# A hybrid stream step on one core: five kept weight units, a fixed order on three engines and grouped transpositions between output and up projection, and another bank for a pool tile

## The chip, the core and the metric

The kernel runs on one core of a Trainium2 chip. Its engines are called as in the profile: PE is TensorE (matrix products; PEld is its weight load), DVE is VectorE, ACT is ScalarE, POOL is GpSimd, SP is SyncE, which here only issues transfers. The metric is the device time of one execution in microseconds (us). Time before is the median of three executions.

## The reference, cut to what matters

One layer is computed for 384 tokens (256 of a prompt and 128 of eight running streams), with a model width of 2048 and a hidden width of 8192:

```python
u = rmsnorm(x, g_mix_pre);  proj = u @ w_in        # pool | z | xBC | dt | gates
a_pool = pool_mixer(...)                           # windows 2, 4, 8, 16
a_ssd  = gated_rmsnorm(ssd_scan(...), z)
m = sigmoid(gA) * (a_pool @ w_pool_proj) + sigmoid(gB) * (a_ssd @ w_ssd_proj)
x = x + rmsnorm(m @ w_out, g_mix_post)             # output projection
x = x + rmsnorm(square(relu(rmsnorm(x, g_mlp_pre) @ w_up)) @ w_down, g_mlp_post)
```

The change lies almost wholly in the last two lines, between `m @ w_out` and the first products with `w_up`. No result of `w_up` can be had before the norm over a token's whole row of `m @ w_out` is known.

## The kernel before, in words

**Products.** Every 32-bit operand is split in a high and a low part, `h` and `l`. A weight unit is 128 x 1024 numbers (512 KB): SP loads it (`wfetch`, L62 to L65), ACT rounds it to `wh` (L72), DVE subtracts to get `wl` (L74). There are three buffers each for the raw unit, `wh` and `wl`. One product is three PE instructions (`mm3`, L80 to L83): `wh` with the high part, `wh` with the low part, `wl` with the high part. `half` (L89) does eight such products with one unit, `proj` (L98) two or more units into one result tile.

**Result tiles.** There are eight banks: two are called `mm` (pool `psm`), six `ss` (pool `pss`). A tile waits until its bank has been read empty.

**Who orders the instructions.** The program is written in order, but a planner places the instructions on each engine by its own costs and due times; it may move one past another on the same engine where the data allow. Each engine then runs its list strictly in that order. `behind(ins)` pins the instructions in it after `ins` on the same engine; with `chain[0]` set, `half` pins each set of products after `last[0]`. Weight splits are not pinned, save the two that `hold` governs: the splits for the second half of up tile 0 and for up tile 1, which `gate` keeps behind the last square root on ACT and a residual on DVE.

**Pool tiles near the start.** Pool tiles 0, 1 and 2 are accumulated in `ss` banks, tile 3 (`ps3`, L246) and tile 4 in the two `mm` banks. The next product is `gate_a(0)` (`pj_ga`), then `pool_map(0)` (`pw`), which needs the four differences `dh`/`dl` of pool tiles 0 to 3 from ACT and DVE (L325, L326).

**End of the scan.** After the last group the program runs `dside`, `gate_b`, `state`, `gate_b`, and then the last transpositions and products of the scan. `state` (`su`, L668) multiplies `xst`, which makes a way through DRAM.

**Output projection.** `moving` (L845) keeps the activations in PE and streams 512 columns of weights. `w_out` is done in four column blocks `nb` of eight units; each gives three result tiles `o[b]`, one for each block `b` of 128 tokens. For `nb = 3` the last three units are kept (`tail = 3`) and used block after block, so that block 0 is done 36 instructions before block 2. `done(b)` squares and sums `o[b]` on ACT (L910), multiplies it with the norm's weights into `hm` on DVE (L913) and, for `nb = 3`, runs `postnorm` (L879 to L892): a root on ACT and eight small instructions on DVE. Ten residuals `x1 += hm * y` follow on DVE (L925), 512 columns each, and two on ACT and POOL (L922, L923).

**To the up projection.** For each of 16 slices `k` of 128 columns, PE transposes the three token blocks of `x1` into one `ss` bank (`trm`, L935), ACT scales and rounds to `x1h` (L939), DVE gets `x1l` (L940). These feed the 64 up tiles `pj_up`, each 48 PE instructions of 384 columns. The norm before the up projection is applied to its results: twelve squares (L951), three `postnorm`, a diagonal `dg` (L955), a product with ones (`bc`, L957, two instructions) and a copy to `r2` (L958). The first reader of an up tile (`ht`, L979) needs `r2`. `bc` lies ahead of up tile 2 in PE's order.

Of the kernel before, what the change touches and what calls it, by code (L numbers as in the profile page):

```python
# [34 lines left out]
def build(ctx, tc, io):  # L35
# [31 lines left out]
    def wsplit(f):  # L67
        w, name = f
        h = wpool.tile([P, 1024], F32R, tag="wh", name=f"wh_{name}")
        l = wpool.tile([P, 1024], F32R, tag="wl", name=f"wl_{name}")  # L70
        with behind(hold[0]):
            s.activation(h, w, AF.Copy)  # L72
        with behind(hold[1]):
            v.tensor_tensor(l, w, h.bitcast(F32), ALU.subtract)  # L74
        return h, l

    def wload(src, name):
# [160 lines left out]
    for k in range(2, KD, 2):  # L238
# [205 lines left out]
    with tc.tile_pool(name="phd", bufs=2, reuse_waits="tile") as pd, tc.tile_pool(  # L444
# [278 lines left out]
        for g in range(G + 1):  # L723
            if g == G:
                dside(prev.p[1])
                gate_b()
                state(prev.p[1])
                gate_b()
                py = sstile("pp_last")
                lump(lambda: t_yT(prev.p[1]))  # L730
                lump(lambda: t_Y(prev.p[1]))
                lump(lambda: t_pp(prev.p[1], py))
                final(prev.p[1])
                gate_b()
# [107 lines left out]
    x1 = res.tile([P, 3, DM], F32, name="x1")  # L842
    r2 = res.tile([P, T], F32, name="r2")

    def moving(o, units, lhs, tail, done, pool=None):  # L845
        nk = len(lhs)

        def mm(b, wh, wl, k, k2):
# [5 lines left out]
            te.matmul(o[b], ml, wh[:, c], start=False, stop=k == nk - 1)  # L854
# [7 lines left out]
        w = [wload(*units[kp]) for kp in range(n - tail, n - max(0, tail - 3))]  # L862
        for kp in range(n - max(0, tail - 3), n):
# [33 lines left out]
    with tc.tile_pool(name="phf", bufs=1, side="right", reuse_waits="tile") as pf, tc.tile_pool(  # L897
# [1 line left out]
    ) as pf2:  # L899
        hm = pf.tile([P, 3, DM], F32, name="hm")  # L900
        st = pf.tile([P, 3, 4], F32, name="st1")
        ys = []
        for nb in range(4):
            gpo = pf2.tile([P, 512], F32, tag="gpo", name=f"gpo{nb}")
            sy.dma_start(gpo, io["g_mix_post"][blk(nb)].partition_broadcast(P))
            o = [sstile(f"wo{nb}_{b}") for b in range(3)]

            def done(b):
                q = pf2.tile([P, 512], F32, tag="q", name=f"q1_{nb}_{b}")
                s.activation(q, o[b], AF.Square, accum_out=st[:, b, nb : nb + 1])  # L910
                if nb == 3:
                    ys.append(postnorm(pf2, st, b, "n1"))
                v.tensor_tensor(hm[:, b, blk(nb)], o[b], gpo, ALU.mult)  # L913

            moving(o, [(io["w_out"][nb, kp], f"wo{nb}_{kp}") for kp in range(8)], ms_, 3 if nb == 3 else 0, done)
        gate = [root[0], None]
        for i in range(4):
            for b in range(3):
                xb = x1[:, b, blk(i)]
                if b == 1 and i >= 2:  # L920
                    hb = hm[:, b, blk(i)]
                    s.activation(hb, hb, AF.Copy, scale=ys[b])  # L922
                    gp.tensor_tensor(xb, xb, hb, ALU.add)  # L923
                    continue
                ins = v.scalar_tensor_tensor(  # L925
                    out=xb, in0=hm[:, b, blk(i)], scalar=ys[b], in1=xb, op0=ALU.mult, op1=ALU.add
                )
            if i == 0:
                gate[1] = ins
    pga = ctx.enter_context(tc.tile_pool(name="pga", bufs=1, reuse_waits="tile"))  # L930
    xs2 = []
    for k in range(KD):
        tr = sstile(f"trm{k}")
        for b in range(3):
            te.transpose(tr[:, b * P : b * P + P], x1[:, b, k * P : k * P + P], ident)  # L935
        h = pga.tile([P, T], F32R, name=f"x1h{k}")
        l = pga.tile([P, T], F32R, name=f"x1l{k}")
        g1 = vec[:, V_GMLP + k : V_GMLP + k + 1]
        s.activation(h, tr[:, :T], AF.Copy, scale=g1)  # L939
        v.scalar_tensor_tensor(out=l, in0=tr[:, :T], scalar=g1, in1=h.bitcast(F32), op0=ALU.mult, op1=ALU.subtract)  # L940
        xs2.append((h, l))
    mpool.close()

    with tc.tile_pool(name="phg", bufs=1, reuse_waits="tile") as pg, tc.tile_pool(
        name="phg2", bufs=2, reuse_waits="tile"
    ) as pg2:
        st = pg.tile([P, 3, 4], F32, name="st2")
        for b in range(3):
            for i in range(4):
                q = pg2.tile([P, 512], F32, tag="q3", name=f"q2_{b}_{i}")  # L950
                s.activation(q, x1[:, b, blk(i)], AF.Square, accum_out=st[:, b, i : i + 1])  # L951
        dg = pg.tile([P, 3, P], F32, name="dg2")
        for b in range(3):
            y = postnorm(pg2, st, b, "n2")
            v.tensor_scalar(dg[:, b, :], ident, y, None, ALU.mult)  # L955
        bc = sstile("bc2")
        te.matmul(bc[:, :T], ones, dg.rearrange("p b t -> p (b t)"), start=True, stop=True)  # L957
        s.copy(r2, bc[:, :T])  # L958
# [5 lines left out]
        pg.tile([P, 96], F32, name="pad_e")  # L964
        NC = 8
        for c8 in range(NC):
            hh = []
            for f8 in range(8):
                f = c8 * 8 + f8
                if f == 0:  # L970
                    ps = mmtile("pj_up0")[:, :T]
                    half(ps, 0, wload(io["w_up"][0, 0], "up0_0"), xs2)
                    hold[:] = gate
                    half(ps, 1, wload(io["w_up"][0, 1], "up0_1"), xs2)
                else:
                    ps = proj([io["w_up"][f, 0], io["w_up"][f, 1]], xs2, f"up{f}")
                    hold[:] = [None, None]
                t = pg2.tile([P, T], F32, tag="t", name=f"ht{f}")
                v.scalar_tensor_tensor(out=t, in0=ps, scalar=0.0, in1=r2, op0=ALU.max, op1=ALU.mult)  # L979
                s.activation(t, t, AF.Square)  # L980
# [5 lines left out]
            for nb in range(4):  # L986
                o = [sstile(f"wd{c8}_{nb}_{b}") for b in range(3)]

                def done(b):
# [10 lines left out]
                        v.tensor_tensor(dst, dst, gpo[:, blk(nb)], ALU.mult)  # L1000
                        return
                    if b == 0:
                        pg.tile([P, 32], F32, name="pad_z")
# [14 lines left out]
                    4 if c8 == NC - 1 and nb == 3 else 0,  # L1018
                    done,
                    pg,  # L1020
                )


# [117 lines left out]
```

## Time and profile before

| what | us |
|---|---|
| median of three executions (2834.87 to 2838.39) | 2836.21 |
| profiled execution, its own time | 2834.49 |
| its span, from the first to the last instruction | 2832.7 |
| PE busy in the span | 2812.7 (99%) |
| DVE, ACT, POOL busy | 1562.9, 1092.0, 96.6 |
| granted PE clock, mean of the span | 0.998 |

Times in a timeline are counted from the start of the span. Matmuls overlap: a matmul of 384 columns is shown with 0.33 us but the next begins 0.173 us later, one of 512 columns is shown with 0.39 us and the next begins 0.227 us later, so work on PE is counted by starts. An "idle" in brackets stands ahead of the instruction that ended it, with what released it.

### The profile page before, as it was taken

The page shows a single profiled execution, that of the slowest core. Times are in us where ns is not written, and L with a number is a line of the kernel's source. Part 1 is how long each engine was busy: PE and PEld are TensorE (multiplying, and loading weights), DVE is VectorE, ACT ScalarE, POOL GpSimd, SP SyncE. Part 2 cuts the span into 40 slices and gives each one's busy share as a digit, 9 for nine tenths or more (in the row PEclk, how much of TensorE's full clock was granted, in tenths as well). Part 3 has the DMA queues.
Part 4 walks back from the last instruction along what each step waited for, and adds up shares of the span by engine and source line. Part 5 has one row for each costly group of instructions (what it writes and reads, how often), then busy time and mean ns, then how long its engine had stood idle before and what let it go on. Part 6 is the DMA issues. An engine that isn't in the chain of part 4 may idle for free.

```text
span 2832.7 us, 39399 instructions
## 1 busy us (share of the span) xinstructions
PE 2812.7 (99%) x15807; PEld 2673.1 (94%) x15807; DVE 1562.9 (55%) x2245; ACT 1092.0 (39%) x1582; POOL 96.6 (3%) x155
## 2 busy tenths in 40 slices
PE   9999999999999999999999999999999999999998
PEld 8999999999999999999999987989899998989897
DVE  6673335687887877886433335434444444444445
ACT  6342224445445445454422234433232333323233
POOL 0000000000000000011000000000000000000000
PEclk9999999999999999999999999999999999999999
DMA  7444445556655665656644543434333343433333
GB/s 263 134 129 141 141 139 193 184 182 203 205 190 193 200 200 190 226 179 229 194 149 149 167 162 111 134 127 127 131 128 127 127 127 129 131 127 127 127 128 125
DMA packets 143494, 451.40 MB, mean 159 GB/s; under 512 B 17296, under 2 KB 43216, under 8 KB 138320
## 3 DMA queue, kind: packets, MB, share of 16 engines
q1 hardware_dynamic: 135056, 412.96, 44.7%
q0 software_dynamic: 8256, 35.93, 3.5%
q8 instruction: 124, 2.03, 0.3%
q14 instruction: 58, 0.48, 0.1%
HBM read 407.11 MB, written 41.72 MB: 158 GB/s over the span
## 4 chain that ended last, share of the span: by engine, by line
PE 98%; DVE 1%; ACT 0%; DMA 0%; issue 0%; SPq 0%; DVEq 0%; ACTq 0%
PE pj_up L83 6%; PE pj_up L81 6%; PE pj_up L82 6%; PE wd L853 6%; PE wd L854 6%; PE wd L852 6%; PE pj_x L81 5%; PE pj_x L83 5%; PE pj_x L82 5%; PE pj_sp L82 3%; PE pj_z L81 3%; PE pj_z L82 3%; PE pj_sp L83 3%; PE pj_z L83 3%; PE pj_sp L81 3%; PE pj_ga L81 2%
## 5 line engine op out<-in xcount | busy, mean ns | idle before, releaser
L83 PE MATMUL pj_up<-x1h,wl_up 128*128 128x384 f32 x1024 | 342.8, 335 | 0.6 <-DVE wl_up L74 0.6
L81 PE MATMUL pj_up<-x1h,wh_up 128*128 128x384 f32 x1024 | 343.0, 335 | 0.0
L82 PE MATMUL pj_up<-x1l,wh_up 128*128 128x384 f32 x1024 | 342.8, 335 | 0.0
L74 DVE TENSOR_TENSOR wl_wd<-w_wd,wh_wd 128x1024 fp32r<-128x1024 f32 x127 | 155.7, 1226 | 261.9 <-ACT wh_wd L72 261.9
L853 PE MATMUL wd<-wl_wd,hh 128*128 128x512 f32 x762 | 296.6, 389 | 0.0
L854 PE MATMUL wd<-wh_wd,hl 128*128 128x512 f32 x762 | 296.6, 389 | 0.0
L852 PE MATMUL wd<-wh_wd,hh 128*128 128x512 f32 x762 | 296.2, 389 | 0.0
L72 ACT ACTIVATE wh_wd<-w_wd 128x1024 fp32r<-128x1024 f32 x127 | 134.8, 1061 | 350.7 <-PE wd L854 284.1
L74 DVE TENSOR_TENSOR wl_up<-w_up,wh_up 128x1024 fp32r<-128x1024 f32 x128 | 156.8, 1225 | 199.6 <-ACT wh_up L72 199.6
L72 ACT ACTIVATE wh_up<-w_up 128x1024 fp32r<-128x1024 f32 x128 | 135.8, 1062 | 326.4 <-PE pj_up L82 265.7
L81 PE MATMUL pj_x<-xgh,wh_x 128*128 128x384 f32 x768 | 257.4, 335 | 0.0
L82 PE MATMUL pj_x<-xgl,wh_x 128*128 128x384 f32 x768 | 256.6, 334 | 0.0
L83 PE MATMUL pj_x<-xgh,wl_x 128*128 128x384 f32 x768 | 256.6, 334 | 0.0
L83 PEld LDWEIGHTS pj_up<-x1h,wl_up 128*128 128x128 f32 x1024 | 192.3, 188 | 1.0 <-DVE wl_up L74 0.9
L81 PEld LDWEIGHTS pj_up<-x1h,wh_up 128*128 128x128 f32 x1024 | 192.5, 188 | 0.4
L82 PEld LDWEIGHTS pj_up<-x1l,wh_up 128*128 128x128 f32 x1024 | 192.5, 188 | 0.3
L81 PE MATMUL pj_z<-xgh,wh_z 128*128 128x384 f32 x512 | 171.1, 334 | 0.0
L83 PE MATMUL pj_z<-xgh,wl_z 128*128 128x384 f32 x512 | 171.1, 334 | 0.0
L853 PEld LDWEIGHTS wd<-wl_wd,hh 128*128 128x128 f32 x762 | 143.0, 188 | 29.7 <-DVE wl_wd L74 0.2
L854 PEld LDWEIGHTS wd<-wh_wd,hl 128*128 128x128 f32 x762 | 143.0, 188 | 29.7
L82 PE MATMUL pj_z<-xgl,wh_z 128*128 128x384 f32 x512 | 171.0, 334 | 0.0
L81 PE MATMUL pj_sp<-abh,wh_sp 128*128 128x384 f32 x512 | 171.0, 334 | 0.0
(305 smaller groups left out, 6088.0 us busy)
## 6 DMA issues: line engine op xcount, KB each, us to landing
w_up<-w_up SPq DMA_DIRECT2D x128, 512.0 KB, 3.4
w_wd<-w_down SPq DMA_DIRECT2D x128, 512.0 KB, 3.4
w_x<-w_in SPq DMA_DIRECT2D x96, 512.0 KB, 4.3
w_z<-w_in SPq DMA_DIRECT2D x64, 512.0 KB, 3.5
w_sp<-w_ssd SPq DMA_DIRECT2D x64, 512.0 KB, 3.5
w_ga<-w_in SPq DMA_DIRECT2D x32, 512.0 KB, 3.5
w_pp<-w_pp SPq DMA_DIRECT2D x32, 512.0 KB, 3.4
hs<-ssm SPq DMA_DIRECT2D x16, 1024.0 KB, 6.2
```

Of the source, the lines that this page charges most:

```text
L72: s.activation(h, w, AF.Copy)
L74: v.tensor_tensor(l, w, h.bitcast(F32), ALU.subtract)
L81: te.matmul(out, wh, xh, start=first, stop=False)
L82: te.matmul(out, wh, xl, start=False, stop=False)
L83: return te.matmul(out, wl, xh, start=False, stop=last)
L852: te.matmul(o[b], mh, wh[:, c], start=k == 0, stop=False)
L853: te.matmul(o[b], mh, wl[:, c], start=False, stop=False)
L854: te.matmul(o[b], ml, wh[:, c], start=False, stop=k == nk - 1)
```

## The change

Six things are edited.

1. Pool tile 3 is accumulated in an `ss` bank.
2. At the end of the scan both `gate_b` run before `state`.
3. In the last block of `w_out` five units are kept instead of three, all five with split tiles of their own (`own = 5`, pool `phk`), so that the three `wh`/`wl` buffers are free for three `w_up` units. The norm's weights are scaled by -0.5 on ACT, which makes `postnorm` one instruction shorter on DVE. Blocks 0 and 1 get their residuals, and block 0 its squares, as soon as they are done; all residuals are on DVE.
4. Transpositions are split into early ones (blocks 0 and 1, two slices to a bank, eight groups) and late ones (block 2, four slices to a bank, four groups), and so are the scalings that read them.
5. Up tiles 0 and 1 are computed together, slice by slice, with `hold` and `gate` gone; PE's order is pinned by `chain`, ACT's by `act`, DVE's by `dve`. Up tile 2 goes to an `ss` bank.
6. `bc` goes between the halves of up tile 2 and uses a high and a low part with rounded ones. The `pad` tiles change size so that later tiles keep their places.

```diff
-    hold = [None, None]
+    tail_pe = [None]
...
-        with behind(hold[0]):
-            s.activation(h, w, AF.Copy)
-        with behind(hold[1]):
-            v.tensor_tensor(l, w, h.bitcast(F32), ALU.subtract)
+        s.activation(h, w, AF.Copy)
+        v.tensor_tensor(l, w, h.bitcast(F32), ALU.subtract)
...
-    ps3 = mmtile("pj_p3")[:, :T]
+    ps3 = sstile("pj_p3")[:, :T]
...
                 dside(prev.p[1])
                 gate_b()
+                gate_b()
                 state(prev.p[1])
-                gate_b()
                 py = sstile("pp_last")
...
+            s.activation(gpo, gpo, AF.Copy, scale=-0.5)
             o = [sstile(f"wo{nb}_{b}") for b in range(3)]
             def done(b):
...
                 v.tensor_tensor(hm[:, b, blk(nb)], o[b], gpo, ALU.mult)
+                if nb < 3:
+                    return
+                ys[b] = postnorm(pf2, st, b, "n1", doubled=True)
+                if b == 2:
+                    return
+                for i in range(4):
+                    residual(b, i)
+                if b == 1:
+                    with behind(root[0]):
+                        for i in range(4):
+                            square(0, i)
+            moving(o, ..., 5 if nb == 3 else 0, done, pk, 5 if nb == 3 else 0)
...
+        ups = [mmtile(f"pj_up{n}")[:, :T] for n in range(2)]
+        uw = {n: wload(io["w_up"][n, q], f"up{n}_{q}") for n, q in ((0, 0), (1, 0))}
+        uw[2] = wload(io["w_up"][0, 1], "up0_1")
+        chain[0] = True
+        last[0] = lastwo
...
+        A, L = [early_turn(j) for j in range(5)], []
+        dve(lambda: residual(2, 0))
+        L.append(late_turn(0))
+        for g in range(4):
+            ks = range(4 * g, 4 * g + 4)
+            for k in ks:
+                hi(k, False)
+            if g:
+                act(lambda: square(1, g - 1))
+            for pair in ((ks[:2], ks[2:]) if g == 0 else (ks,)):
+                for k in pair:
+                    lo(k, False)
+                for k in pair:
+                    hi(k, True)
+                for k in pair:
+                    lo(k, True)
+            if g < 3:
+                dve(lambda: residual(2, g + 1))
+            def more():
+                A.append(early_turn(5 + g))
+                L.append(late_turn(g + 1))
+            if g == 0:
+                for k in ks:
+                    for n in range(2):
+                        prod(n, (k,), uw[n])
+                    if k == 2:
+                        more()
+            elif g == 1:
+                for k in (4, 5):
+                    for n in range(2):
+                        prod(n, (k,), uw[n])
+                more()
+                prod(0, (6, 7), uw[0])
+                prod(1, (6, 7), uw[1])
+                uw[3] = wload(io["w_up"][1, 1], "up1_1")
+            else:
+                for k in ks:
+                    prod(0, (k,), uw[2])
+                    if k == 10:
+                        more()
+        prod(1, range(8, KD), uw[3])
+        chain[0] = False
+        for b, i in ((1, 3), (2, 0), (2, 1), (2, 2), (2, 3)):
+            act(lambda: square(b, i))
...
+        ups.append(sstile("pj_up2")[:, :T])
+        half(ups[2], 0, wload(io["w_up"][2, 0], "up2_0"), xs2)
+        bc = sstile("bc2")[:, :T]
+        with behind(last[0]):
+            te.matmul(bc, onesr, dgh.rearrange("p b t -> p (b t)"), start=True, stop=False)
+            last[0] = te.matmul(bc, onesr, dgl.rearrange("p b t -> p (b t)"), start=False, stop=True)
+        with behind(last[0]):
+            half(ups[2], 1, wload(io["w_up"][2, 1], "up2_1"), xs2)
+        s.copy(r2, bc)
...
-                if f == 0:
-                    ps = mmtile("pj_up0")[:, :T]
-                    half(ps, 0, wload(io["w_up"][0, 0], "up0_0"), xs2)
-                    hold[:] = gate
-                    half(ps, 1, wload(io["w_up"][0, 1], "up0_1"), xs2)
-                else:
-                    ps = proj([io["w_up"][f, 0], io["w_up"][f, 1]], xs2, f"up{f}")
+                ps = ups[f] if f < 3 else proj([io["w_up"][f, 0], io["w_up"][f, 1]], xs2, f"up{f}")
```

`turn` (called by `early_turn` and `late_turn`) transposes the given token blocks of the given slices into one bank, pinned after `last[0]`. `hi(k, late)` is ACT's scaling of the two early blocks (256 columns) or of the late one (128 columns) of slice `k`, `lo(k, late)` DVE's difference for the same columns; `prod(n, ks, w)` is `mm3` for up tile `n` and the slices `ks`. Each is pinned after the one before it on its engine. The removed code is that of L918 to L941 and L948 to L958, told above.

More of the change, by code (lines that the diff above doesn't have):

```diff
@@ L843, in build, with moving @@
     r2 = res.tile([P, T], F32, name="r2")
-    def moving(o, units, lhs, tail, done, pool=None):
+    def moving(o, units, lhs, tail, done, pool=None, own=0):
         nk = len(lhs)
@@ L853, in mm @@
             te.matmul(o[b], mh, wl[:, c], start=False, stop=False)
-            te.matmul(o[b], ml, wh[:, c], start=False, stop=k == nk - 1)
+            tail_pe[0] = te.matmul(o[b], ml, wh[:, c], start=False, stop=k == nk - 1)
         n = len(units)
@@ L861, in moving @@
                     mm(b, wh, wl, kp * 2 + k2, k2)
-        w = [wload(*units[kp]) for kp in range(n - tail, n - max(0, tail - 3))]
-        for kp in range(n - max(0, tail - 3), n):
+        w = [wload(*units[kp]) for kp in range(n - tail, n - own)]
+        for kp in range(n - own, n):
             f, name = wfetch(*units[kp])
@@ L901, in build, with residual, square @@
         st = pf.tile([P, 3, 4], F32, name="st1")
-        ys = []
+        st2 = pf.tile([P, 3, 4], F32, name="st2")
+        phk = ExitStack()
+        pk = phk.enter_context(tc.tile_pool(name="phk", bufs=1, reuse_waits="tile"))
+        ys = [None] * 3
+        def residual(b, i):
+            xb = x1[:, b, blk(i)]
+            return v.scalar_tensor_tensor(
+                out=xb, in0=hm[:, b, blk(i)], scalar=ys[b], in1=xb, op0=ALU.mult, op1=ALU.add
+            )
+        def square(b, i):
+            q = pf2.tile([P, 512], F32, tag="q", name=f"q2_{b}_{i}", bufs=1)
+            return s.activation(q, x1[:, b, blk(i)], AF.Square, accum_out=st2[:, b, i : i + 1])
         for nb in range(4):
@@ L930, in build @@
[L930 to L941, printed above, removed]
+                if nb < 3:
+                    return
@@ new lines, in done @@
+                ys[b] = postnorm(pf2, st, b, "n1", doubled=True)
[7 more added lines that the diff above has]
+                            square(0, i)
+            moving(
+                o,
+                [(io["w_out"][nb, kp], f"wo{nb}_{kp}") for kp in range(8)],
+                ms_,
+                5 if nb == 3 else 0,
+                done,
+                pk,
+                5 if nb == 3 else 0,
+            )
@@ new lines, in build @@
+            lastwo = tail_pe[0]
+        phk.close()
+        pga = ctx.enter_context(tc.tile_pool(name="pga", bufs=1, reuse_waits="tile"))
+        xs2 = [
+            (pga.tile([P, T], F32R, name=f"x1h{k}"), pga.tile([P, T], F32R, name=f"x1l{k}")) for k in range(KD)
+        ]
+        ups = [mmtile(f"pj_up{n}")[:, :T] for n in range(2)]
+        uw = {n: wload(io["w_up"][n, q], f"up{n}_{q}") for n, q in ((0, 0), (1, 0))}
+        uw[2] = wload(io["w_up"][0, 1], "up0_1")
+        chain[0] = True
@@ new lines, in build, with turn, go, act @@
+        last[0] = lastwo
+        rt2 = root[0]
+        def turn(o, blocks, ks):
+            def go():
+                j = 0
+                for k in ks:
+                    for b in blocks:
+                        i = te.transpose(o[:, j * P : j * P + P], x1[:, b, k * P : k * P + P], ident)
+                        j += 1
+                return i
+            with behind(last[0]):
+                last[0] = go()
+        ca, cd = [rt2], [None]
+        def act(fn):
+            with behind(ca[0]):
+                ca[0] = fn()
@@ new lines, in dve, with part, hi @@
+        def dve(fn):
+            with behind(cd[0]):
+                cd[0] = fn()
+        def part(k, late):
+            i = k % 4 if late else k % 2
+            o = L[k // 4] if late else A[k // 2]
+            t = slice(TP, T) if late else slice(0, TP)
+            n = P if late else TP
+            g1 = vec[:, V_GMLP + k : V_GMLP + k + 1]
+            return o[:, i * n : i * n + n], xs2[k][0][:, t], xs2[k][1][:, t], g1
+        def hi(k, late):
+            src, h, l, g1 = part(k, late)
+            act(lambda: s.activation(h, src, AF.Copy, scale=g1))
@@ new lines, in lo, with early_turn, late_turn @@
+        def lo(k, late):
+            src, h, l, g1 = part(k, late)
+            dve(
+                lambda: v.scalar_tensor_tensor(
+                    out=l, in0=src, scalar=g1, in1=h.bitcast(F32), op0=ALU.mult, op1=ALU.subtract
+                )
+            )
+        def early_turn(j):
+            o = sstile(f"trm{j}")
+            turn(o, (0, 1), (2 * j, 2 * j + 1))
+            return o
+        def late_turn(i):
+            o = sstile(f"trl{i}")
+            turn(o, (2,), range(4 * i, 4 * i + 4))
+            return o
@@ new lines, in build @@
+        prod(1, range(8, KD), uw[3])
+        chain[0] = False
+        for b, i in ((1, 3), (2, 0), (2, 1), (2, 2), (2, 3)):
+            act(lambda: square(b, i))
+        dgh = pf.tile([P, 3, P], F32R, name="dgh2")
+        dgl = pf.tile([P, 3, P], F32R, name="dgl2")
+        with behind(cd[0]):
+            for b in range(3):
+                y = postnorm(pf2, st2, b, "n2")
+                v.tensor_scalar(dgh[:, b, :], ident, y, None, ALU.mult)
+                v.scalar_tensor_tensor(
+                    out=dgl[:, b, :], in0=ident, scalar=y, in1=dgh[:, b, :].bitcast(F32), op0=ALU.mult, op1=ALU.subtract
+                )
@@ L946, in build @@
     ) as pg2:
[L947 to L958, printed above, removed]
         hacc = pg.tile([P, 3, DM], F32, name="hacc")
@@ L1020, in build @@
                     pg,
+                    1 if c8 == NC - 1 and nb == 3 else 0,
                 )
```

30 lines of the change are left out of this document (11 added, 19 removed).

## The prediction

> **What bounds the kernel now.** I read the page's first part and its chain, then PE's waits, then the timelines of PE, DVE and ACT around each wait, and the clock there by stretch. PE works or is fed all the time:
>
> ```profile
> PE 2812.7 (99%) x15807; PEld 2673.1 (94%) x15807; DVE 1562.9 (55%) x2245; ACT 1092.0 (39%) x1582; POOL 96.6 (3%) x155
> ...
> PE 98%; DVE 1%; ACT 0%; DMA 0%; issue 0%; SPq 0%; DVEq 0%; ACTq 0%
> ```
>
> The change takes away no product, so it can only win where PE waits or runs slowly. PE's whole list of waits in the middle of the span is short:
>
> ```profile
> PE pj_ga L81 <- DVE pbuf L291: 3.5, 1, 3.5
> PE trm L935 <- DVE x L925: 2.4, 2, 2.0
> ...
> PE bc L957 <- DVE dg L955: 1.3, 1, 1.3
> PE su L668 <- DMA xst<-x_scr: 1.0, 1, 1.0
> PE pj_up L83 <- DVE wl_up L74: 0.6, 1, 0.6
> PE trm L935 <- DVE hm L913: 0.4, 1, 0.4
> ...
> PE trm L935 <- DVE x1l L940: 0.3, 1, 0.3
> ```
>
> Five of these seven are at the boundary from output to up projection and make 5.0 us; the pool tile has 3.5, the scan's end 1.0. The clock by stretch (columns: busy times, then the granted clock, DMA share, GB/s) shows one more loss:
>
> ```profile
> 1756.00:1758.00 2.00, 0.07 (x1) 0.00 (x0) 1.93 (x4) 1.37 (x2) 1.26 (x2) 0.81 0.08 33
> 1758.00:1760.00 2.00, 1.89 (x8) 1.67 (x8) 2.00 (x5) 1.37 (x3) 0.00 (x0) 0.50 0.00 0
> ...
> 1762.00:1764.00 2.00, 2.00 (x10) 1.85 (x9) 2.00 (x5) 1.53 (x5) 0.00 (x0) 0.50 0.98 406
> 1764.00:1766.00 2.00, 2.00 (x18) 1.93 (x16) 1.68 (x4) 1.78 (x4) 0.00 (x0) 0.99 0.20 82
> ```
>
> After the gap the granted clock is 0.50 for about 6.4 us. So I measure the boundary as a whole. ACT starts to read the last `w_out` tile at 1753.38; DVE reads up tile 2 at 1793.46:
>
> ```profile
> 1785.14 0.56 DVE L979 SCALAR_TENSOR_TENSOR ht<-pj_up,r 128x384 f32<-128x384 f32 x1 [1.55 <-PE pj_up L83]
> 1793.46 0.56 DVE L979 SCALAR_TENSOR_TENSOR ht<-pj_up,r 128x384 f32<-128x384 f32 x1 [2.02 <-PE pj_up L83]
> ```
>
> Both reads come 0.2 behind PE's last start, so the stretch is **40.1 us**, from 1753.18 (called T) on. Needed in it: three up tiles at 8.32 (the distance of these two rows), 24.96; 48 transpositions at 0.113 (three of them and a matmul take 0.51 in the timeline, less 0.173), 5.4; `bc` 0.4. That is 30.8, so 9.3 us are waits, slow clock and filling: the most that the boundary can give.
>
> **The change part by part, boundary.** *Ahead of T.* With five kept units block 1 ends 30 matmuls, 6.8 us, before T instead of 4.1. Its square, root, norm and four residuals of 0.67 take about 4.7 (block 0 now: 1745.2 to 1750.5 with three residuals and the table load of 1.3), so blocks 0 and 1 are ready before T. The five splits (1.06 on ACT, 1.23 on DVE each) need no PE release any more; by the issue times now (one unit each 4.08, landing in 3.4) the last is split some 20 us before T, and its first use is 15 before T. Hidden: ACT waits 3.0 of each 4.08 there. Four scalings of the norm's weights cost ACT 0.6 each in the same waits; the table load before the first root (1.28) stays ahead of T.
>
> *Block 2.* DVE's part after the root is what kept PE waiting:
>
> ```profile
> 1756.18 1.10 DVE L891 TENSOR_TENSOR n_n<-n_n,n_n 128x1 f32<-128x1 f32 x1
> 1757.31 1.41 DVE L925 SCALAR_TENSOR_TENSOR x<-hm,n_n,x 128x512 f32<-128x512 f32 x2
> ```
>
> L891 takes 0.15 elsewhere; here 1.10, while POOL's residual (1754.77 to 1757.26) runs, which the change drops, as it drops ACT's two scalings (0.71 each) ahead of the root. With the spacings of block 1 (square 0.7, root 0.3, DVE steps 0.2, 0.3, 0.2) the first residual starts at T+2.0 and ends at T+2.7, not T+4.9. PE fills this with 20 early transpositions: 0.138 each when alone (five in 0.69), 2.76; then four late ones, 0.55.
>
> *First product.* ACT's late scaling of slice 0 (128 columns; an estimate of 0.40 from 0.58 for 384 and 0.60 for 512) ends at T+3.9, DVE's difference at T+4.3. PE has done the transpositions at T+3.3, so 0.8 is idle. Now the first product starts at T+6.1 and then drips.
>
> *Pace after that.* A slice gives PE 1.04 (two tiles, six matmuls of 0.173). ACT needs 0.40 and 0.31 per slice, DVE 0.40 and 0.27, so both keep up, with three squares, four residuals and two or three splits in between. Where a late group is transposed, ACT and DVE need 0.3 to 0.7 until the next product. I follow the order group by group: groups 1 and 2 meet PE at about the time at which it is ready; in group 4 the early scalings of slices 14 and 15 wait for a transposition that PE does only after slice 10, a square stands behind them, and slice 12 comes 1.0 late. With a split of 1.06 on ACT in a bad place, 1.5.
>
> *Sum.* 3.3 + 0.8 + 24.96 + 24 transpositions at 0.13 (3.1) + `bc` 2 x 0.17 (0.35) + 1.5 = **34.0**. `bc` no longer waits: squares and norm end near T+25, PE asks for it at T+29. Gain **6.0**; bounds 3.5 (each of four groups 0.6 worse) and 7.5 (no group late).
>
> **Pool tile.** `pj_ga` could not start at 48.6 since both `mm` banks were held and DVE read tile 3 only at 51.7. With tile 3 elsewhere `pj_ga` runs at once. What is late next is `pool_map`, behind the same DVE:
>
> ```profile
> 56.80 0.55 DVE L326 TENSOR_TENSOR dl<-d,dh 128x384 fp32r<-128x384 f32 x1
> 57.27 0.69 DVE L306 TENSOR_TENSOR win<-win 128x516 f32<-128x516 f32 x1
> 57.88 1.22 DVE L74 TENSOR_TENSOR wl_pw<-w_pw,wh_pw 128x1024 fp32r<-128x1024 f32 x1
> ```
>
> `pj_ga` ends at 56.9; the fourth slice is wanted nine matmuls later, at 58.5; DVE has it at 57.3. The second `wl_pw` is wanted at 61.1 and there at 59.1. So the wait goes: gain **3.2** (lower bound 1.5, if the planner puts a window sum of 0.69 and a split of 1.22 ahead; upper 3.5). Six `ss` banks hold three pool tiles, tile 3 and `bc_x`; none is waited for.
>
> **Scan's end.** With 8.3 us more, `xst` is there: 1.0 goes. The second gate's units are split in time (1264.9 and 1278.7 for uses at 1275.9 and 1280.1). But the last transposition needs a seventh bank right behind `su`, so it waits for DVE's first state addition, perhaps behind a gate's product (0.55): 0.3. Gain **0.7**, bounds -0.3 and 1.0.
>
> **Sum.** 6.0 + 3.2 + 0.7 = 9.9. The profiled execution would go from 2834.5 to 2824.6; it lies 1.7 below the median of the runs, so the median would go from 2836.2 to **2826.3**.
>
> [...] The row is the 0.50 clock above, after 4.9 us with twelve transpositions and waits. A gap of 3.5 without any PE work (48.6 to 52.1) left the clock at 1.00, so the row alone doesn't say whether transpositions count. [...] No run here shows 24 transpositions in a row.
>
> **Rivals.**
> 1. *The clock halves after the 24 transpositions*, for 3.4 to 6.4 us (the row). Half of it is lost: 1.7 to 3.2, so 2828.0 to 2829.5. For: the row. Against: no gap over 0.7 is left, and the clock came back at 1764 after four products of 0.32 in 3.2 us. [...] 14%.
> 2. *The pool wait comes back as `pool_map` on DVE*, which is 9.9 of 10 us busy from 50 to 60: 1.7 lost, 2828.0. 8%.
> 3. *The order isn't what it says*: weight splits, `bc`'s copies and the scaling of `g_mlp_post` (1.92 on ACT) are not pinned; where the planner sets them between pinned ones, ACT blocks until PE frees a buffer. About 1.2 to 1.9 in each of three groups and half of the pool's gain gone: 2830.5 to 2835. 13%.
> 4. *Slower*: the clock stays at 0.50 through all four groups, since the products now come in lumps between transpositions. About 20 us of PE work (16.6 of products, 3.1 of transpositions) take twice as long: +18, less 9.9, so 2844. It decides from ten such microseconds on. Against: at 1760.8 to 1764 the products were sparser, and the clock rose. 5%.
>
> **How the numbers follow.** The forecast has 60%, at 2826.3. The low end takes all upper bounds (7.5 + 3.5 + 1.0 = 12.0) and 0.7 for the spread of the runs: 2823.5. The high end takes in rivals 1 and 2 and the edge of 3: 2831. About 2 in 10 are left out. 0.2% is 5.7 us, about what a measurement here can tell: faster by that is the forecast with rivals 1 and 2, 82%; within it rival 3, 13%; slower 5%.
>
> **What would show it.** Right: no wait of `pj_ga` on L291, none of `su` on `xst`; first residual of block 2 near T+2.0; first up product near T+4; `ht` of up tile 2 near T+34; clock 1.00 throughout. Wrong: a clock of 0.50 behind T, ACT waiting on PE ahead of a weight split within T to T+20, or a new wait of `pw` on `dl`.

## The result, and the profile after

The changed kernel takes **2826.31 us** (median of six executions, 2825.35 to 2827.09) against 2836.38 for the kernel before (six, 2834.87 to 2838.39): ratio 0.9964, 95% interval 0.9951 to 0.9977. The profiled execution took 2827.09, with a span of 2825.2, so it is one of the longer ones. The forecast was 2826.3. The number came out, but not all of its terms: the boundary gave less than forecast, the scan's end more, and in the medians the pool tile more too.

The page shows the same PE work in a shorter span:

```profile
PE 2811.2 (100%) x15807; PEld 2673.2 (95%) x15807; DVE 1565.7 (55%) x2263; ACT 1096.2 (39%) x1600; POOL 94.3 (3%) x153
...
PE 98%; DMA 1%; DVE 0%; ACT 0%; SPq 0%; issue 0%; DVEq 0%; ACTq 0%
```

The waits of PE after the change (total, times, longest). `pj_ga`, `su` and `bc` have left the list; apart from the first weights (`wh_e`, below), what stands in their place is all at the boundary and makes 2.9:

```profile
PE trl L963 <- DVE x L907: 1.1, 2, 0.9
...
PE pj_up L81 <- DVE wl_up L72: 0.7, 1, 0.7
PE pj_up L80 <- DVE x1l L995: 0.6, 2, 0.4
PE pj_up L79 <- ACT x1h L990: 0.5, 1, 0.5
```

The timeline of PE from T on (T is 1749.02 here, 0.2 before ACT's read of the last `w_out` tile at 1749.22) shows one block of 20 transpositions, a wait, four late ones, a wait, and the first product at T+4.3:

```profile
1748.96 2.34 PE L963 MATMUL trm<-cst,x 128*128 128x128 f32 x20
1752.17 0.66 PE L963 MATMUL trl<-cst,x 128*128 128x128 f32 x4 [0.86 <-DVE x L907]
1753.28 0.45 PE L79 MATMUL pj_up<-x1h,wh_up 128*128 128x384 f32 x1 [0.46 <-ACT x1h L990]
1753.93 0.45 PE L80 MATMUL pj_up<-x1l,wh_up 128*128 128x384 f32 x1 [0.20 <-DVE x1l L995]
```

The clock by stretch (the 0.59 and 0.56 stand behind the busy times): it was 1.00 through the 24 transpositions and fell 1.1 behind the start of the first product.

```profile
1754.00:1756.00 2.00, 2.00 (x8) 2.00 (x9) 2.00 (x6) 1.83 (x6) 0.00 (x0) 0.59 0.00 0
1756.00:1758.00 2.00, 2.00 (x8) 2.00 (x8) 1.67 (x5) 0.86 (x3) 0.00 (x0) 0.56 0.00 0
```

The same stretches in a second execution of the changed kernel (`e0_after`, below), in which the clock didn't fall:

```profile
1754.00:1756.00 2.00, 2.00 (x12) 2.00 (x13) 2.00 (x7) 1.86 (x6) 0.00 (x0) 1.00 0.00 0
1756.00:1758.00 2.00, 2.00 (x16) 1.97 (x15) 1.64 (x5) 0.83 (x3) 0.00 (x0) 1.00 0.00 0
```

DVE's side, with the read of up tile 2 at the end (the row that stood at 1793.46 before):

```profile
1749.94 0.69 DVE L924 TENSOR_TENSOR hm<-wo,gpo 128x512 f32<-128x512 f32 x1 [2.70 <-ACT q L923]
...
1751.37 0.75 DVE L907 SCALAR_TENSOR_TENSOR x<-hm,n_n,x 128x512 f32<-128x512 f32 x1
...
1786.05 0.56 DVE L1099 SCALAR_TENSOR_TENSOR ht<-pj_up,r 128x384 f32<-128x384 f32 x1 [0.19 <-PE pj_up L81]
```

**Where the time went.** Four marks cut the span: the first product `pw` of `pool_map` (its weight load), the first of the SSD projection `pj_sp` behind the scan, ACT's read of the last `w_out` tile, DVE's read of up tile 2. The last column is `e0_after`.

| stretch, us | before | after | after, clock 1.00 |
|---|---|---|---|
| start to `pw` (pool tile) | 60.4 | 57.4 | 57.4 |
| `pw` to `pj_sp` (end of the scan) | 1295.8 | 1294.6 | 1294.5 |
| `pj_sp` to ACT's last read | 397.2 | 397.3 | 397.3 |
| that to up tile 2 (boundary) | 40.1 | 36.8 | 35.3 |
| up tile 2 to the end | 1039.3 | 1039.1 | 1039.3 |
| span | 2832.7 | 2825.2 | 2823.8 |

So the saving sits in the three edited places and nowhere else: 3.0, 1.2, and 3.3 or 4.8. In the first row PE's waits for the early weights (`wh_e`, 0.4 before and 0.9 after) hide 0.5; they differ from execution to execution, from none to 1.3 in the 14 traces.

### The profile page after: what moved, and what is told of

Read it like the earlier page. It is cut to its first block, busy times and chain, and to the rows that moved or that the text cites. A ratio compares the mean times of both kernels' runs of the same rounds, so it can differ in the third digit from the quotient of the medians.

```text
span 2825.2 us, 39432 instructions
## 1 busy us (share of the span) xinstructions
PE 2811.2 (100%) x15807; PEld 2673.2 (95%) x15807; DVE 1565.7 (55%) x2263; ACT 1096.2 (39%) x1600; POOL 94.3 (3%) x153
## 4 chain that ended last, share of the span: by engine, by line
PE 98%; DMA 1%; DVE 0%; ACT 0%; SPq 0%; issue 0%; DVEq 0%; ACTq 0%
PE pj_up L80 6%; PE pj_up L81 6%; PE pj_up L79 6%; PE wd L851 6%; PE wd L852 6%; PE wd L850 6%; PE pj_x L79 5%; PE pj_x L81 5%; PE pj_x L80 5%; PE pj_z L81 3%; PE pj_sp L80 3%; PE pj_sp L79 3%; PE pj_z L79 3%; PE pj_z L80 3%; PE pj_sp L81 3%; PE pj_ga L79 2%
## 5 line engine op out<-in xcount | busy, mean ns | idle before, releaser
L850 PEld LDWEIGHTS wd<-wh_wd,hh 128*128 128x128 f32 x762 | 143.1, 188 | 29.6
```

## The experiments

The theory behind all of them: two things were mis-sized, both by falls of the clock. Behind the pool gap of before, the clock falls in most executions, though not in the profiled one (mean clock 0.997 or less in 32 of 52); behind the short gaps at the first up products of after, it falls in about half of them (0.998 in five of eleven). The rivals are that the parts gain and lose by order and waits alone, and that the transpositions bring the clock down. At the boundary lateness and the clock turn out to count both.

### Each part alone

The pool tile alone (`a1_pool`), the gates alone (`a2_gates`), and the boundary alone (`a3_boundary`: the changed kernel with the other two undone).

```diff
 a1_pool, on the kernel before
-    ps3 = mmtile("pj_p3")[:, :T]
+    ps3 = sstile("pj_p3")[:, :T]
 a2_gates, on the kernel before
                 gate_b()
+                gate_b()
                 state(prev.p[1])
-                gate_b()
```

> The kernel before with one edit alone: pool tile 3 is accumulated in an ss bank. My theory (the bank is what held the first gate product, and the fourth difference of the pool tiles is there 1.2 us before pool_map asks for it): the wait of 3.5 us of pj_ga on L291 goes and nothing takes its place, so about 3.2 us less than before (2833.2). Rival (the wait comes back as pool_map on DVE's differences): at most 1.8 us less, with a wait of pw on dl in PE's list.

> The kernel before with one edit alone: both gate products run ahead of the last state product. My theory: the wait of 1.0 us of su on xst goes, and a wait of about 0.3 us of the next transposition on DVE's state addition (a seventh bank) takes its place: 0.7 us less than before. Rival (banks are the bound there): no gain, or up to 0.3 us more, with the new wait in PE's list.

> The changed kernel with the pool tile and the gate order put back, so the boundary alone. My forecast for it was 6.0 us less than before. The trace of the changed kernel gives 36.9 us from the first transposition to the end of up tile 2, where 34.0 were forecast and 40.1 were needed before: 3.2 us less in that execution, in which the clock stood at 0.5 for 3.4 us. If the clock falls in only some executions, the median should be 3.5 to 5.5 less than before; if it falls in all, 3.2 less.

Measured, each against the 27 executions of before on the same chip (median 2836.79; eleven executions each):

| kernel | median | ratio, 95% | difference |
|---|---|---|---|
| `a1_pool` | 2831.05 | 0.9979, 0.9970 to 0.9988 | -5.7 |
| `a2_gates` | 2836.96 | 1.0001, 0.9992 to 1.0009 | +0.2 |
| `a3_boundary` | 2833.73 | 0.9990, 0.9981 to 0.9998 | -3.1 |

The pool tile's median falls by more than the wait of 3.5 that it removes, though the interval (3.4 to 8.5) just takes in the wait alone. The traces of `a2_gates` and `a3_boundary` have a pool gap as before (3.9 and 3.5), and the clock behind it offers a reason. These are before, and then two rows of `a2_gates`:

```profile
54.00:58.00 4.00, 4.00 (x25) 4.00 (x24) 3.97 (x12) 2.00 (x6) 0.54 (x1) 1.00 0.43 131
...
54.00:56.00 2.00, 2.00 (x8) 2.00 (x8) 2.00 (x6) 0.55 (x2) 0.00 (x0) 0.50 0.10 35
56.00:58.00 2.00, 2.00 (x10) 2.00 (x9) 1.97 (x7) 0.82 (x3) 0.42 (x1) 0.68 0.90 262
```

In these 4 us PE starts 16 or 18 products (by the window asked for) where the profiled execution of before, at clock 1.00, starts 25: 1.2 to 1.5 us lost. The prediction saw one execution in which that fall was absent. With the 3.5 that makes about 5 where every execution falls; the rest of the 5.7 isn't explained, and isn't clear of noise. The gates' gain doesn't show in this median (the interval allows -2.3 to +2.6), but it does in the marks: `pw` to `pj_sp` is 1295.7 or 1295.8 in the four kernels with the old order, and 1294.5 or 1294.6 in all ten traces with the new one. In the trace of `a2_gates` the first row is 2.1 longer than before and the boundary 0.9, which hides it.

The boundary alone gives 3.1 (interval 0.6 to 5.4). That is below the 6.0 of the forecast, and below the 3.5 to 5.5 that I expected for a clock that falls in part of the executions, which the interval doesn't exclude. The three differences make -8.6, the whole change -10.1; with intervals this wide, that the parts add up is neither shown nor refuted.

### The pool gap filled with products that nobody reads

```diff
 d1_gapfill, on the kernel before, between pool tile 4 and gate_a(0)
+                        fo = sstile("fill")[:, :T]
+                        with behind(last[0]):
+                            for _ in range(18):
+                                ins = te.matmul(fo, xg[0][0][:, :P], xg[0][0], start=True, stop=True)
+                        last[0] = ins
+                        chain[0] = True
                         sg = gate_a(0)
+                        chain[0] = False
```

The other lines pin the order: unread products behind pool tile 4, `gate_a(0)` behind them.

> The kernel before with one addition: in PE's gap ahead of the first gate product 18 products of 384 columns, whose result nobody reads (3.1 us of PE work in a gap of 3.5; the gate product still waits for its bank). The pool tile alone gave 5.7 us at the median, though the wait it takes away is 3.5. Theory (the gap lets the granted clock fall to 0.5 for 3.4 us in most executions, which costs 1.7 to 2.2 more): the wait stays, the clock stays at 1.00 from 44 to 66 us in every execution, and the time is 1.5 to 2.2 us less than before. Rival (the other 2.2 us come from DVE's order, not from the clock): no change.

Measured: 2835.25 (2833.79 to 2836.05, eleven) against 2836.58 (15), ratio 0.9994, 0.9985 to 1.0003. `pj_ga` starts no earlier (`pw` at 60.8), and the clock in its trace stays at 1.00 from 44 to 70. The difference of 1.3 is about what a fall costs, but the interval includes zero, so the size isn't shown by this alone. The mean clocks are plainer. Of 52 executions of before, 11 have a mean of 0.996 (median time 2838.5), 21 of 0.997 (2836.9), 20 of 0.998 (2836.2). All eleven of `a2_gates`, with the gap, have 0.997. Without the pool gap (`a1_pool`) or with it filled (`d1_gapfill`), 17 of 22 have 0.998, five 0.999, none less. The third digit is a rough sign: a fall to half for 3.4 us takes 0.0006 off the mean, and the half clock at the end, behind PE's last product, lasts 3.7 us in the trace of before and 5.9 in that of after, which moves it by 0.0004. But none of 22 against 32 of 52 is no accident of rounding: the pool gap brings falls in most executions of before.

### Do transpositions bring the clock down?

The first five early groups are transposed five times over: 80 more transpositions, the same data.

```diff
 c2_turns, on the kernel after
-            turn(o, (0, 1), (2 * j, 2 * j + 1))
+            for _ in range(5 if j < 5 else 1):
+                turn(o, (0, 1), (2 * j, 2 * j + 1))
```

> The changed kernel with each of the five first early groups transposed five times over: 100 transpositions in a row instead of 20, about 11.7 us at 0.117 each, then all as in the changed kernel. If transpositions count as work for the clock, it stays at 1.00 through them, and the span is 8.5 to 9.5 us longer than the changed kernel's. [...]

Measured: one execution, 2833.27, span 2831.4, which is 7.6 above the clean execution of after. I had expected 8.5 to 9.5; the 80 more took 8.7, and the wait of 0.86 that stood behind the 20 is gone. PE did nothing but transpositions for 10.9 us, at 0.11 each:

```profile
1749.06 11.08 PE L963 MATMUL trm<-cst,x 128*128 128x128 f32 x100
1759.98 0.60 PE L963 MATMUL trl<-cst,x 128*128 128x128 f32 x4
1761.04 0.45 PE L79 MATMUL pj_up<-x1h,wh_up 128*128 128x384 f32 x1 [0.46 <-ACT x1h L990]
```

and the clock stayed up, during and behind them:

```profile
1756.00:1760.00 4.00, 4.00 (x39) 4.00 (x38) 0.00 (x0) 0.00 (x0) 0.00 (x0) 1.00 0.00 0
1760.00:1764.00 4.00, 3.35 (x20) 2.85 (x19) 2.73 (x8) 2.71 (x9) 0.00 (x0) 1.00 0.02 4
```

So it isn't the transpositions that bring the clock down here, as rival 1 has it: 100 of them in a row, of 128 x 128 in 32 bits, left it at 1.00. It is one execution.

### The boundary's gaps filled

Five products that nobody reads (each starts its tile anew, and the first real one does so again) stand ahead of the late transpositions, three behind. The transpositions are untouched.

```diff
 b1_fill, on the kernel after (fill(n) is n products of 384 columns into ups[0])
         dve(lambda: residual(2, 0))
+        fill(5)
         L.append(late_turn(0))
+        fill(3)
```

> The changed kernel with eight products of 384 columns, whose result nobody reads, in PE's two gaps at the boundary: five between the early and the first late transpositions (0.87 of 0.86 us), three behind the late ones (0.52 of 0.46). Theory (the gaps and the transpositions let the clock fall in about half of the executions, at 1.6 us each): the clock stays at 1.00 at the boundary, all times lie at the lower end of the changed kernel's, and the median is 0.5 to 1.0 us less. Rival (transpositions don't count as work, and eight products are too few): as often a clock of 0.5 as in the changed kernel, and the median 0 to 0.4 more.

> The changed kernel as it is, once more, so that the others of this set can be compared with it in the same runs. If the granted clock falls behind the short gaps at the first up products only in part of the executions, its runs lie in two groups some 1.2 to 1.6 us apart, with mean clocks of 0.998 and 0.999, and its median is 2826.3 plus or minus 0.7. If the clock has nothing to do with the spread, times and mean clocks are not linked.

Measured: `b1_fill` 2825.51 (2825.33 to 2826.64, five; ratio 0.9960, 0.9947 to 0.9972), and the changed kernel once more, `e0_after`, 2826.43 (2825.53 to 2827.02, five; ratio 0.9961, 0.9949 to 0.9974). The same two waits, filled:

```profile
1751.24 1.13 PE L1004 MATMUL pj_up<-wh_up 128*128 128x384 f32 x5
1752.34 0.66 PE L963 MATMUL trl<-cst,x 128*128 128x128 f32 x4
1752.76 0.77 PE L1004 MATMUL pj_up<-wh_up 128*128 128x384 f32 x3
1753.46 0.45 PE L79 MATMUL pj_up<-x1h,wh_up 128*128 128x384 f32 x1
```

The first real product comes no sooner (T+4.3), and the boundary takes 35.3, as in the clean execution of after. So the fill is worth nothing in itself; it keeps the clock up. Six of the eleven executions of the changed kernel have a mean clock of 0.999 and a median of 2825.7, five have 0.998 and 2826.9. All ten with the fill (`b1_fill` and `e2_fill_early`) have 0.999, median 2825.5. As the third digit is rough, 0.999 doesn't exclude a fall; the times say more: nine of the ten with the fill lie between 2825.3 and 2825.9, the tenth at 2826.6, and of the eleven without it four lie below 2825.9. With the transpositions the same in all and the gaps of 0.86 and 0.46 filled (the 0.20 is there in both), the falls go with the idle gaps, not with the transpositions, in about half of the executions, for about 1.2 us each time.

### Three kept units instead of five

```diff
 b2_keep3, on the kernel after, last call of moving for w_out (tail and own)
-                5 if nb == 3 else 0,
+                3 if nb == 3 else 0,
...
-                5 if nb == 3 else 0,
+                3 if nb == 3 else 0,
```

> The changed kernel with three kept units instead of five in the last block of the output projection, still with tiles of their own. Block 1 then ends 4.1 us before the last product instead of 6.8, and its norm and four residuals (about 4.2 on DVE) end 0.3 to 0.8 after it, which holds up the third to fifth early group. Theory (five units are needed): first product at T+4.6 to T+5.3 instead of T+4.2, 0.3 to 1.2 us slower than the changed kernel. Rival (block 2's own chain ends last anyway): the same time.

Measured: 2827.29 (2827.09 to 2827.95, four; ratio 0.9966, 0.9952 to 0.9979), about 0.9 over the changed kernel, which was measured at other times. DVE is still at block 1's residuals when block 2 is done, so `hm` starts 0.8 later behind T, and everything after it:

```profile
1747.91 2.74 DVE L907 SCALAR_TENSOR_TENSOR x<-hm,n_n,x 128x512 f32<-128x512 f32 x4
1750.57 0.69 DVE L924 TENSOR_TENSOR hm<-wo,gpo 128x512 f32<-128x512 f32 x1
```

PE waits 1.7 instead of 0.9 for the first residual, and the first product comes at T+5.1. The clock falls in this trace as in that of after, so the two compare: two more kept units buy 0.8 of the boundary's gain, not more.

### What makes slice 12 late

`a4_pin` pins the weight split for up tile 2 behind the last late scaling, and that tile's first half behind the last product of up tile 1; `e2_fill_early` (with the fill) issues the last group of transpositions one slice earlier.

```diff
 a4_pin, on the kernel after
-        chain[0] = False
+        with behind(ca[0]), behind(cd[0]):
+            wu2 = wload(io["w_up"][2, 0], "up2_0")
...
-        half(ups[2], 0, wload(io["w_up"][2, 0], "up2_0"), xs2)
+        half(ups[2], 0, wu2, xs2)
+        chain[0] = False
 e2_fill_early, on b1_fill
-                    if k == 10:
+                    if k == 9:
```

> The changed kernel, with the first half of up tile 2 and the split of its unit pinned behind the last product of up tile 1 and behind the last scalings. In the changed kernel the planner put four products of up tile 2 between those of slices 11 and 12 of up tile 0, and PE stood 0.74 us there for that unit's low part, which DVE makes ahead of four late differences. Theory (unpinned filling costs): 0.7 to 1.2 us less than the changed kernel, and no wait of pj_up on a weight split. Rival (slice 12 would have been late by as much anyway): no difference of over 0.3 us, and the wait is then on x1h or x1l.

> The changed kernel with the eight unread products in the gaps of the boundary, and with the last group of transpositions one slice earlier (behind slice 9, not 10). The unread products alone gave 2825.5. Theory A, slice 12 is late because PE transposes slices 14 and 15 too late for ACT: ACT gets them 0.5 us earlier, and 0.3 to 0.5 us go, 2825.0 to 2825.2. Rival B, DVE's last residual of block 2 and the weight splits set that time: PE waits 0.5 longer for that residual, nothing is gained, 2825.5, and DVE's difference of slice 12 starts no earlier against the start of the stretch.

Measured: `a4_pin` 2826.29 (2825.84 to 2828.82, five; ratio 0.9965, 0.9953 to 0.9978), nothing gained; `e2_fill_early` 2825.55 (2825.41 to 2825.89, five; ratio 0.9959, 0.9946 to 0.9971), nothing over `b1_fill`. My theory fell both times. In `a4_pin` PE stands idle in front of slice 12 instead of working ahead on up tile 2:

```profile
1768.47 0.44 PE L79 MATMUL pj_up<-x1h,wh_up 128*128 128x384 f32 x1 [0.36 <-ACT x1h L990]
1769.63 0.45 PE L80 MATMUL pj_up<-x1l,wh_up 128*128 128x384 f32 x1 [0.72 <-DVE x1l L995]
```

In the changed kernel the planner does products of up tile 2 there and then waits 0.74 for that tile's `wl`: the same microsecond in another place. In `e2_fill_early` the earlier transpositions wait 0.78 instead of 0.26 for DVE's last residual. DVE's difference of slice 12 starts at 20.4 behind ACT's read of the last `w_out` tile with the early group and without it: from 1764 on, in `b1_fill`, DVE has late differences, a split, a residual, four early differences and another split ahead of it without a gap. But DVE isn't alone. In `a4_pin` the second of these splits is out of the way, and DVE waits for ACT instead, so that the difference starts at 20.15, only 0.3 earlier:

```profile
1769.22 1.13 DVE L995 SCALAR_TENSOR_TENSOR x1l<-trl,vec,x1h 128x128 fp32r<-128x128 f32 x4 [0.77 <-ACT x1h L990]
```

So two chains end at nearly the same time: DVE's with that split, and ACT's, which had waited for the last group of transpositions. Each run eased one of them. Both eased together were not run, so what that would gain is open.

### The order on ACT and DVE, and the two tiles together

`b3_nopins` leaves ACT's and DVE's order to the planner; `b4_single` does up tiles 0 and 1 one after the other.

```diff
 b3_nopins, on the kernel after
-            with behind(ca[0]):
-                ca[0] = fn()
+            ca[0] = fn()
...
-            with behind(cd[0]):
-                cd[0] = fn()
+            cd[0] = fn()
 b4_single, on the kernel after (groups 0 and 1; tile 1 follows whole at the end)
-                    for n in range(2):
-                        prod(n, (k,), uw[n])
+                    prod(0, (k,), uw[0])
```

> The changed kernel without the fixed order on ACT and DVE in the up tiles 0 and 1; PE's order stays fixed. Theory A, the order is worth something: the planner sets squares or scalings of later slices ahead of the late scalings, PE waits for x1h or x1l 1 to 3 us more, 2827 to 2829.5. Rival B, the planner's own order does the same: 2826.3 within 0.7, and it could even avoid the weight split that stands ahead of slice 12.

> The changed kernel with up tiles 0 and 1 one after the other. A slice then gives PE 0.52 us of products while ACT needs 0.71 and DVE 0.67 of scalings for it, so theory A is that PE starves through the first tile: the late scalings of four groups set the pace, 2.5 to 3.5 us more than with two tiles together, 2829 to 2830, with waits of PE for x1h and x1l of 3 us or more in sum and the clock below 1 longer. Rival B, the transpositions between the groups give ACT and DVE time enough: under 1 us more, 2826.3 to 2827.3.

Measured, beside `e0_after` with 2826.43: `b3_nopins` 2828.09 (2826.81 to 2828.77, six; ratio 0.9968, 0.9956 to 0.9980), `b4_single` 2827.97 (2826.52 to 2828.40, five; ratio 0.9966, 0.9954 to 0.9979). Without the order the first residual waits behind scalings and differences that nobody needs yet, and later slices come late by 0.72 and 1.46; the boundary takes 36.97, 1.7 more, at clock 1.00:

```profile
1752.97 0.66 PE L963 MATMUL trl<-cst,x 128*128 128x128 f32 x4 [1.78 <-DVE x L907]
...
1767.76 0.44 PE L80 MATMUL pj_up<-x1l,wh_up 128*128 128x384 f32 x1 [1.46 <-DVE x1l L993]
```

With one tile at a time PE waits for DVE's differences four times instead of twice (total, times, longest), and the boundary takes 37.3, 2.0 more:

```profile
PE pj_up L80 <- DVE x1l L995: 2.0, 4, 0.7
```

That is less than I expected. ACT and DVE did lag at the start of each group, as the expectation said, but the transpositions between the groups let them catch up in part. Both parts are worth something, about 1.5 to 2 us each, in five or six executions.

## Why the prediction was right, and where not

**Pool tile, 3.2.** The wait of `pj_ga` is gone and none has come in its place. Rival 2 did not come: `pool_map` runs without a wait, though the planner did put a window sum and a split ahead of the third and fourth differences. In the traces the wait's 3.5 are saved. In the medians `a1_pool` gives 5.7 (3.4 to 8.5): the step that failed is in the part on the 0.50 clock, where the prediction took the clock of 1.00 behind the pool gap for a property of the kernel and so priced the gap at its length alone. It was one of the executions without a fall. For the same reason the shift of 1.7 from profile to median was not a constant: by the mean clocks much of it was this fall, and the change removes it.

**Scan's end, 0.7.** In the traces 1.2, in ten alike. The 0.3 that I took off for the seventh bank did not come: PE has no wait there. About 1.0 is the wait for `xst`; where the other 0.2 come from I did not settle.

**Boundary, 6.0.** 4.8 with the clock up, 3.3 in the profiled execution, 3.1 in the medians of `a3_boundary`; of these only the first lies within the bounds of the forecast (3.5 and 7.5). Of its own signs, the first residual and the first product came near the forecast, `ht` of up tile 2 came at T+37.0 (T+35.5 with the clock up) and not at T+34, and a clock of 0.50 behind T, which it had named as a sign of being wrong, was there in the profiled execution. Step by step:

- *Ahead of T* held: blocks 0 and 1 are ready, and 20 transpositions start at once.
- *Block 2*: the first residual starts at T+2.35 and ends at T+3.1, forecast 2.0 and 2.7. `hm` on DVE waits until ACT's square has read the same tile and its sum is out (1749.22 to 1749.91; `hm` at 1749.94), so the root ends at 1750.23, but DVE's first step on it starts at 1750.55. The prediction's steps leave `hm` out and did not see that the two readers take turns. In the trace 0.03 us lie between them, and what released `hm` was ACT's read.
- *First product*: T+4.3, forecast 3.9 to 4.3. The transpositions took 2.34, forecast 2.76, which only lengthened the wait.
- *Pace after that*: this is the step that failed, a term that was too small. From the first product to up tile 2 the clean execution takes 31.0; products, `bc` and three groups of eight transpositions (0.79 each) make 27.7. The other 3.3 are lost by lateness, where I had allowed 1.5: 0.5 at the first difference, 0.5 in group 2, 0.5 at the last late transpositions, 1.0 in front of slice 12, and 0.8 for slow starts, since behind each wait or group of transpositions the product after the first starts 0.26 to 0.28 later, not 0.173. The transpositions were 0.7 cheaper than forecast. Slice 12 came 1.0 late, as forecast, but by way of a wait for up tile 2's `wl`.
- *Clock*: rival 1, at 14%, happened in about half of the executions. Its size was 1.2 us in the medians and 1.5 in the profile (ten products at 0.32 instead of 0.173), not 1.7 to 3.2, and it went with the idle gaps (`b1_fill`), not the transpositions (`c2_turns`). What was held against it, that no gap over 0.7 is left, was not so: one of 0.86 was. (The 3.4 us in its bounds stood in no row of before, where the 0.50 lasted 6.8, from 1757.23 to 1764.05; the trace of after has 3.4, from 1754.36 to 1757.77.)
- *Order*: rival 3's mechanism is there in small: two unpinned splits on DVE stand ahead of late differences. What that costs isn't shown, since `a4_pin`, with one of them out of the way, gained nothing; it is at most the 1.0 at slice 12, not half of the gain. Rival 4 did not happen.

**The sum.** From the profile of before to a clean execution of after the span went from 2832.7 to 2823.8: -8.9, forecast -9.9. Before's median lies 1.9 above its profiled execution, and after's 0.6 above the median of its clean ones (2825.7). So the median went down by 10.1. That the forecast of 9.9 was so close is luck: two errors of about one microsecond had opposite signs. The span of a clean execution went down 1.0 less than forecast, mainly by the pace at the boundary, with the clock up; the shift from a clean execution to the median became 1.3 smaller, by the mean clocks mostly through the falls.

**Fastest.** `b1_fill` and `e2_fill_early`, at 2825.5, are a little below both kernels, with no fall of the clock in their traces and nothing else gained.

## What to carry to other kernels

One profiled execution shows a clock that may differ in the next; before pricing a gap on a saturated PE, look at times and mean clocks of several executions, and price the gap as its length plus what a fall behind it may cost, here 1.2 to 1.5 us (`a2_gates`, after). Work ahead of a late operand can be worth as much as making it early: two tiles together hid some 2 us here. Where two engines' chains end at nearly the same time (here DVE's and ACT's at slice 12), easing one alone gains nothing. If gaps can't be closed, products that nobody reads held the clock at 1.00 here at no cost (`b1_fill`, 2825.51 against 2826.43).

## What the runs showed of the hardware

**The length of a gap alone didn't say whether the clock falls.** The same 3.5 us were followed by 1.00 in one trace and by 0.50 in another, and so were the same three short gaps:

| trace | PE idle, us | clock behind |
|---|---|---|
| before, pool gap | 3.5 | 1.00 |
| `a3_boundary`, pool gap | 3.5 | 0.50 |
| `a2_gates`, pool gap | 3.9 | 0.50 |
| after, boundary | 0.86, 0.46, 0.20 | 0.50 |
| `e0_after`, boundary | 0.86, 0.46, 0.21 | 1.00 |
| `b3_nopins`, boundary | 1.78, 0.55, 0.20 | 1.00 |
| `b2_keep3`, boundary | 1.68, 0.46, 0.20 | 0.50 |

At the boundary the 0.50 lasted 6.8 us in the trace of before and 3.4 in that of after. What decides between the two outcomes isn't shown: no run moved a gap on purpose.

- **Transpositions of 128 x 128 kept the clock up** (`c2_turns`: 100 in a row, 1.00 during and behind them) and cost 0.11 each in a block.
- **Two readers of one result tile took turns here**, ACT first (1749.22 to 1749.91 in the trace of after) and DVE 0.03 behind its end, though neither writes it.
